# A hybrid decoder layer on one core: a new order of the seven block products, and the attention groups combined inside the attention stages

## The chip, the cores and the metric

The kernel runs on one core of a Trainium2 chip. The metric is the device time of one execution in microseconds. Before the change it is 3054.38 us, the median of three runs (3054.3 to 3061.18).

## What is computed

The reference is one decoder layer over a prompt of 2048 tokens and over eight sample sequences of one new token each, with model width 1024. After an RMS norm, one input projection feeds two branches, which are merged by sigmoid gates, projected and added to the residual:

```
h = rms_norm(x)
for g, (win, dil) in enumerate(((128, 1), (512, 4), (2048, 16))):   # 8 heads of 64 each
    q, k, v = cols(h, w_in, ...)            # 512 columns each
    o[g], lse[g] = dilated_attn(q, k, v, win, dil, alibi_slopes[g])   # 129 keys per query
mix = softmax over g of lse                 # per position and head
att = sum_g mix[g] * o[g] * silu(cols(h, w_in, OFF_ATT_GATE, 512))
# HGRN2 branch, 8 heads: q, f, i, gate of 1024 columns each
S_t = diag(f_t) S_{t-1} + k_t i_t^T;   o_t = S_t^T q_t     (evaluated in chunks)
ho = rms_norm(o) * silu(gate)
merged = ga * (att @ w_att_proj) + gb * (ho @ w_hg_proj)   # ga, gb: sigmoid of 1024 columns each
y = rms_norm(x + merged @ w_out)
```

All of it is float32. New keys and values, the HGRN state and the sample outputs are returned too.

## The kernel before

**Products.** A float32 operand is split into two parts of a faster type, `hi` and `lo` (`split_w`: ScalarE writes `hi`, VectorE subtracts to get `lo`), and a product is three matmuls per 128 rows of depth: hi*hi, hi*lo and lo*hi. On top of that each projection is a two-by-two block product done with seven block products instead of eight. The 1024 rows of depth are the two blocks of one side. The tokens of a half (1024) are split in two 512s, and two column groups are the blocks of the other side. `ORDER` names the seven combinations of the token side (`A11`, `S1`, `S2`, `A12`, `S3`, `S4`, `A22`; all seven stay in SBUF for a half), `w_combos` makes the seven of the weight side from four raw tiles and one difference tile (`wr`, five buffers). So product i multiplies `ORDER[i]` with `W[i]`. Before, the order is P1, P5, P6, P2, P7, P3, P4, where P1 + P2 is the first result block and the other three need sums of partial results that are kept aside.

**Two layouts.** `nat_block` computes values and HGRN inputs with tokens on the partitions (two accumulator banks for each of the three tags `pa`, `pb`, `pc`). The kept partial sums are copied by ScalarE (`keep_c`, tile `cc`), the results are added by VectorE or copied by ScalarE into `vst` and stored (`nat_fin`). `t_pair` computes everything else with columns on the partitions, two groups of 128 columns at a time, with one bank for each tag; tags `pa` and `pb` change places from one column block to the next (`flip`). In the first half (p = 0) a pair runs as two column blocks of 256 and 260 tokens (the four extra are sample tokens), in the second (p = 1) as one of 512. Both blocks of a pair use the same seven weights `W`. `open_T(slots, raws)` sets how many split weights the pool holds: 7 in the first half, 5 in the second.

**Stages.** Natural blocks of the first half; `att_stage(0)`, `cb_stage(0)`, `hg_stage(0)`; the token side of the second half is loaded and split; natural blocks of the second half, with the whole sample attention and sample HGRN state work handed in between the products (`mid`); then `att_stage(1)`, `cb_stage(1)`, `hg_stage(1)`, and two output stages.
- `att_stage` runs over four pairs of heads j and three groups g. `att_proj` projects q and k (a `t_pair`); `att_side` of the pair before does scores, Exp, transposes and the weighted values, and stores the outputs with their maxima and denominators to `natt[g][j]` in DRAM. Its score tiles `sc` have three buffers.
- `cb_stage` runs the two gate pairs (`att_gates`, Sigmoid, stored to `gs_scr`) and two merge-gate pairs (`merge_pair`), and for each j `combine`: it loads the three groups (`na`, 512 positions a tile), computes the softmax weights over the groups on VectorE with one Exp on ScalarE, scales and adds. `combine_T` transposes the result on TensorE, multiplies it by the gate read back from `gs_scr` (tile `gc`) and stores it to `att_scr`.
- `hg_stage` alternates per head a pair for f and q (`hg_fq`, with `hg_decay` behind it), the chunk recurrence of the head before (`hg_side`) and a pair for the gates.

**What sets the order.** The program is written in the order above, but a scheduler orders each engine's instructions: it goes by priority, which is program order unless `high_priority` lifts it (the weight splits of the next pair are lifted), and lets a later instruction go first where an earlier one would wait for data, a buffer or a bank. The order it finds is fixed; each engine then takes its queue in order. All loads and stores of these stages are issued from SyncE's queue. Buffers of a tag are given to a new tile when the old one's last reader is done.

Of the kernel before, what the change touches and what calls it, by code (L numbers as in the profile page):

```python
# [10 lines left out]
F32 = mybir.dt.float32  # L11
# [7 lines left out]
P = 128  # L19
# [23 lines left out]
HC = HALF // P  # L43
SW = 512 + NS // 2
SETS = (((0, 256), (256, 260)), ((0, 512),))
ORDER = ("A11", "S1", "S2", "A12", "S3", "S4", "A22")
C_IDENT, C_STEPS, C_STEPS2, C_CAUSAL, C_ONES, C_SEL, C_W = 0, 128, 384, 512, 640, 768, 776


# [27 lines left out]
def body(ctx, tc, x_p, x_s, c128, c512, c2048, st_in, norm_w, w_in, w_ap, w_hp, w_out, hg_nw, lbl, fin_w,  # L77
# [7 lines left out]
    sto = nc.sync.dma_start  # L85
# [146 lines left out]
    def w_combos(pl, raws, width, bufs, slots):  # L232
        def slot(src):
            return w_slot(pl, src, width, slots)

        b11, b21, b12, b22 = raws[0, 0], raws[1, 0], raws[0, 1], raws[1, 1]
        w0 = slot(b11)
        t3 = pl.tile([P, 4, width], F32, name="wr", tag="wr", bufs=bufs)
        V.tensor_tensor(out=t3, in0=b22, in1=b12, op=ALU.subtract)
        V.tensor_tensor(out=b12, in0=b12, in1=b11, op=ALU.subtract)  # L240
        w1 = slot(b12)
        V.tensor_tensor(out=b11, in0=b22, in1=b12, op=ALU.subtract)
        w2 = slot(b11)
        w3 = slot(b21)
        w4 = slot(t3)
        V.tensor_tensor(out=b21, in0=b21, in1=b11, op=ALU.subtract)
        w5 = slot(b22)
        w6 = slot(b21)
        return [w0, w1, w2, w3, w4, w5, w6]
# [61 lines left out]
                sto(kv[o0:o0 + (2 - u0) * P].rearrange("(u p) c -> p u c", p=P), v[:, u0:])  # L311

    def nat_fin(wn, p, g, half, r, c, b, ps, add):
        v = wn.tile([P, 2, 256], F32, name="vst", tag="vst", bufs=2)
        vf = v.rearrange("p u c -> p (u c)")
        if add is None:
            A.copy(out=vf, in_=ps)
        else:
            V.tensor_tensor(out=vf, in0=ps, in1=add, op=ALU.add)
        nat_store(p, g, half, r, c, b, v)  # L320
# [7 lines left out]
    def nat_block(wn, p, g, half, mid=None):  # L328
        raws = w_raw(wn, nat_cols(g, half), 256, 5)
        if p == 0:  # L330
            nat_samp(wn, raws, g, half)
        W = w_combos(wn, raws, 256, 5, 3)

        def prod(ps, b, i, first):
            for u in range(2):
                nat_mm(ps[:, u * 256:(u + 1) * 256], Hh[ORDER[i]], Hl[ORDER[i]], *W[i],
                       slice((2 * b + u) * P, (2 * b + u + 1) * P), first and u == 0, True)

        def keep_c(ps):
            c = wn.tile([P, 512], F32, name="cc", tag="cc", bufs=4 + p)  # L340
            A.copy(out=c, in_=ps)
            return c

        pa, pb, pc = [[ps_proj(t) for _ in range(2)] for t in range(3)]
        cc = {}
        for i, t in enumerate((pa, pc, pa, pb, pa, pc, pa)):
            for b in range(2):
                prod(t[b], b, i, i in (0, 1, 3))
                if i < 3:
                    cc[i, b] = keep_c(t[b])  # L350
                else:
                    r, c, add = ((0, 0, 0), (1, 1, 1), (0, 1, 2), (1, 0, None))[i - 3]
                    nat_fin(wn, p, g, half, r, c, b, t[b], None if add is None else cc[add, b])
            for f in mid.pop(0) if mid else ():
                f()
# [43 lines left out]
    def t_pair(p, c0s, idx, evs, W=None):  # L399
        W = W or t_combos(c0s)  # L400
        pl = tp["p"]
        for off, n in SETS[p]:
# [15 lines left out]
            def keep_c(ps):  # L418
                c = pl.tile([P, 512], F32, name="cc", tag="cc", bufs=3)
                A.copy(out=c[:, 0:n], in_=ps[:, 0:n])  # L420
                return c
# [9 lines left out]

            prod(pa, 0, True)
            c1 = keep_c(pa)
            prod(pc, 1, True)
            c5 = keep_c(pc)
            prod(pa, 2)
            c2 = keep_c(pa)
            prod(pb, 3, True)
            fin(0, 0, pb, c1)
            prod(pa, 4)  # L440
            fin(1, 1, pa, c5)
            prod(pc, 5)
# [205 lines left out]
            if n < 6:  # L648
                a, b = na, score(n + 3)

    def att_gates(pl, p, j, sto=sto):
        def evac(j):
            def f(r, off, npr, ps, add):
                z = val(ps, add)
                gt = pl.tile([P, 512], F32, name="gm", tag="gm", bufs=3)[:, 0:npr]
                A.activation(out=gt, in_=z, func=AF.Sigmoid)
                V.tensor_tensor(out=gt, in0=z, in1=gt, op=ALU.mult)
                t0 = p * HALF + r * 512 + off
                sto(gs_scr[j][:, t0:t0 + npr], gt)
            return f  # L660

        t_pair(p, (OFF_G + j * P, OFF_G + (j + 1) * P), (48 + j, 49 + j), (evac(j), evac(j + 1)))

    def combine(cb, j, cs):
        pend = []
        for c in cs:
            na = cb.tile([P, 3, 4, 132], F32, name="na", tag="na", bufs=4)
            for g in range(3):
                dma(na[:, g], natt[g][j][c * 512:(c + 1) * 512].rearrange("(i u) c -> i u c", u=4))
            mx = cb.tile([P, 4, 2], F32, name="mx", tag="mx", bufs=2)  # L670
            w3 = cb.tile([P, 3, 4, 2], F32, name="w3", tag="w3", bufs=2)
            V.tensor_tensor(out=mx, in0=na[:, 0, :, 128:130], in1=na[:, 1, :, 128:130], op=ALU.min)
            V.tensor_tensor(out=mx, in0=mx, in1=na[:, 2, :, 128:130], op=ALU.min)
            for g in range(3):
                V.tensor_tensor(out=w3[:, g], in0=mx, in1=na[:, g, :, 128:130], op=ALU.subtract)
            A.activation(out=w3, in_=w3, func=AF.Exp)
            wd = cb.tile([P, 3, 4, 2], F32, name="wd", tag="wd", bufs=2)
            V.tensor_tensor(out=wd, in0=w3, in1=na[:, :, :, 130:132], op=ALU.mult)
            V.tensor_tensor(out=mx, in0=wd[:, 0], in1=wd[:, 1], op=ALU.add)
            V.tensor_tensor(out=mx, in0=mx, in1=wd[:, 2], op=ALU.add)  # L680
# [8 lines left out]
            pend.append((c, na))  # L689
        return j, pend  # L690

    def combine_T(cb, j, pend):
        for c, na in pend:
            pt = ps_side()
            for u in range(4):
                TE.transpose(pt[:, u * P:(u + 1) * P], na[:, 0, u, 0:128], ident)
            gt = cb.tile([P, 512], F32, name="gc", tag="gm", bufs=3)
            dma(gt, gs_scr[j][:, c * 512:(c + 1) * 512])
            V.tensor_tensor(out=gt.rearrange("p (i u) -> p u i", u=4), in0=pt.rearrange("p (u i) -> p u i", u=4),
                            in1=gt.rearrange("p (i u) -> p u i", u=4), op=ALU.mult)  # L700
# [128 lines left out]

    def cb_stage(p):  # L830
        with pool("cb") as cb:
            fill = [lambda j=j: att_gates(cb, p, j) for j in (0, 2)]
            fill += [lambda d=d: merge_pair(cb, p, d) for d in ((0, 2) if p == 0 else (2, 4))]
            for j in range(4):
                if fill:
                    fill.pop(0)()
                if j:
                    combine_T(cb, *pend)
                pend = combine(cb, j, (2 * p, 2 * p + 1))
            for f in fill:  # L840
                f()
            combine_T(cb, *pend)

    def hg_stage(p):
# [307 lines left out]
        return samp_hg_prep, samp_hg_calc, samp_hg_state, samp_hg_out, samp_hg_end  # L1152

    def att_stage(p):
        with pool("at") as at:
            pend = None
            for j in range(4):
                for g in range(3):
                    nxt = (p, j, g) + att_proj(at, p, j, g) if pend is None else None
                    if pend is not None:  # L1160
                        att_side(at, *pend)
                        nxt = (p, j, g) + att_proj(at, p, j, g)
                    pend = nxt
            att_side(at, *pend)

    alloc_H()
    with banks(6, ABC), pool("wn") as wn, right("px") as px:
# [72 lines left out]

    bk = banks(3, ABC)
    bk.__enter__()
    open_T(7, 5)
    att_stage(0)
    cb_stage(0)
    hg_stage(0)
# [243 lines left out]
```

## Time and profile before

| | |
|---|---|
| median of 3 runs | 3054.38 us |
| profiled execution, its own time | 3056.5 us |
| its span, first to last instruction | 3054.6 us |
| TensorE busy | 2884.6 us, 94% |
| TensorE weight loads busy | 2502.7 us, 82% |
| VectorE busy | 1851.9 us, 61% |
| ScalarE busy | 1468.7 us, 48% |
| mean granted clock of TensorE | 0.979 of full speed |
| moved by DMA | 357 MB, mean 117 GB/s |

In the rows below TensorE stands as PE, VectorE as DVE, ScalarE as ACT, SyncE as SP; L413 is line 413 of the kernel. Matmuls overlap: one takes 0.28 us from start to end, but the next starts 0.12 us after it, so busy time is not throughput. PEclk is the share of full speed (2.4 GHz) that was granted to TensorE, which runs at 2.4 or 1.2 GHz. A wait is put down to what came last before it ended.

### The profile page before, as it was taken

Reading aid. Unit: us, or ns where it says so; the run is one execution under the profiler, and the core shown is the slowest. Engines: PE = TensorE matmul, PEld = TensorE weight load, DVE = VectorE, ACT = ScalarE, POOL = GpSimd, SP = SyncE. Lnnn points to the kernel's source line nnn. Section 1 sums busy time; section 2 is a strip of 40 time slices with the busy share of each in tenths; the row PEclk is TensorE's granted clock in tenths of the full one; section 3 lists DMA queues with packets and bytes.
Section 4 is the critical chain, followed back from the end, with each engine's and each line's share of the span. In section 5 each row is a group of like instructions: output and inputs, shape, how many; then the busy total and the mean of one; then the engine's idle time right before and its main releaser. Section 6 shows DMA issues by size and latency. Waiting matters only on the chain. (4 is left out here: it accounts for less than half of the span.)

```text
span 3054.6 us, 54166 instructions
## 1 busy us (share of the span) xinstructions
PE 2884.6 (94%) x20318; PEld 2502.7 (82%) x20318; DVE 1851.9 (61%) x4603; ACT 1468.7 (48%) x3271; POOL 2.5 (0%) x8
## 2 busy tenths in 40 slices
PE   8998999998899999989979999999999999999999
PEld 7997878888898999888866676777788887899886
DVE  7454455557777777666345555558877777544443
ACT  6333454545576676532334444445677773311232
POOL 0000000000000000000000000000000000000000
PEclk9999999999999999999989999999999999999999
DMA  5453222215421222457753222326322224744542
GB/s 188 141 173 112 70 60 82 82 57 173 129 64 60 76 64 83 162 173 242 206 149 87 83 86 79 93 64 205 93 81 73 78 76 151 224 135 136 161 150 78
DMA packets 453362, 357.45 MB, mean 117 GB/s; under 512 B 28505, under 2 KB 411818, under 8 KB 452178
## 3 DMA queue, kind: packets, MB, share of 16 engines
q1 hardware_dynamic: 452482, 351.93, 38.2%
q8 instruction: 162, 2.65, 0.4%
q0 software_dynamic: 320, 1.05, 0.1%
q14 instruction: 110, 0.90, 0.1%
q10 hardware_dynamic: 288, 0.92, 0.1%
HBM read 241.06 MB, written 113.26 MB: 116 GB/s over the span
## 5 line engine op out<-in xcount | busy, mean ns | idle before, releaser
L193 ACT ACTIVATE wh<-wr 128x512 fp32r<-128x512 f32 (+1 forms) x543 | 366.5, 681 | 523.1 <-PE pb L415 196.5
L194 DVE TENSOR_TENSOR wl<-wr,wh 128x512 fp32r<-128x512 f32 (+1 forms) x543 | 405.5, 752 | 240.9 <-ACT wh L193 213.4
L413 PE MATMUL pc<-hhS,wh 128*128 128x256 f32 (+2 forms) x816 | 266.3, 326 | 5.1 <-PEq L1348 3.9
L415 PE MATMUL pc<-hlS,wh 128*128 128x256 f32 (+2 forms) x816 | 264.7, 324 | 0.0
L416 PE MATMUL pc<-hhS,wl 128*128 128x256 f32 (+2 forms) x816 | 264.0, 324 | 0.0
L413 PE MATMUL pa<-hhA,wh 128*128 128x256 f32 (+2 forms) x612 | 204.7, 335 | 24.9 <-ACT gm L707 7.6
L590 ACT ACTIVATE sc<-sc,stg 128x256 f32<-128x256 f32 (+2 forms) x384 | 171.6, 448 | 99.8 <-DVE stg L588 96.5
L413 PE MATMUL pb<-hhA,wh 128*128 128x260 f32 (+2 forms) x612 | 203.9, 333 | 9.6 <-ACT wh L193 4.4
L415 PE MATMUL pa<-hlA,wh 128*128 128x256 f32 (+2 forms) x612 | 200.8, 328 | 0.0
L416 PE MATMUL pa<-hhA,wl 128*128 128x256 f32 (+2 forms) x612 | 200.6, 328 | 0.0
L415 PE MATMUL pb<-hlA,wh 128*128 128x260 f32 (+2 forms) x612 | 200.3, 327 | 0.0
L416 PE MATMUL pb<-hhA,wl 128*128 128x260 f32 (+2 forms) x612 | 198.9, 325 | 0.0
L588 DVE CUSTOM_DVE_ANT_0 sc<-px,bt 128x256 f32<-128x256 f32 (+2 forms) x384 | 123.6, 352 | 124.1 <-PE px L585 39.0
L413 PEld LDWEIGHTS pc<-hhS,wh 128*128 128x128 f32 x816 | 155.1, 190 | 19.4 <-issue 6.9
L193 ACT ACTIVATE th<-ra 128x256 fp32r<-128x256 f32 (+1 forms) x148 | 57.3, 417 | 224.9 <-PE pp L1399 157.4
L415 PEld LDWEIGHTS pc<-hlS,wh 128*128 128x128 f32 x816 | 155.1, 190 | 12.1 <-issue 1.5
L416 PEld LDWEIGHTS pc<-hhS,wl 128*128 128x128 f32 x816 | 155.1, 190 | 11.4 <-issue 0.2
L413 PEld LDWEIGHTS pa<-hhA,wh 128*128 128x128 f32 x612 | 117.6, 192 | 37.6 <-ACT gm L707 9.1
L600 PE MATMUL px<-cm,sc 128*128 128x128 f32 (+1 forms) x600 | 131.1, 294 | 17.0 <-ACT sc L590 15.2
L413 PE MATMUL pb<-hhS,wh 128*128 128x260 f32 (+1 forms) x408 | 136.2, 334 | 8.8 <-ACT cc L420 8.8
L413 PE MATMUL pa<-hhS,wh 128*128 128x256 f32 (+1 forms) x408 | 137.5, 337 | 7.5 <-ACT cc L420 7.5
L416 PE MATMUL pa<-hhS,wl 128*128 128x256 f32 (+1 forms) x408 | 135.9, 333 | 0.0
(476 smaller groups left out, 8319.3 us busy)
## 6 DMA issues: line engine op xcount, KB each, us to landing
wr<-in_w_in SPq DMA_DIRECT2D x272, 256.0 KB
wr<-in_w_in SPq DMA_DIRECT2D x40, 512.0 KB
vt<-vscr SPq DMA_DIRECT2D x52, 256.0 KB
na<-natt SPq DMA_DIRECT2D x48, 264.0 KB
vscr<-vst SPq DMA_DIRECT2D x48, 256.0 KB
natt<-stg SPq DMA_DIRECT2D x32, 264.0 KB
xt<-in_x_prompt SPq DMA_DIRECT2D x16, 512.0 KB
iscr<-vst SPq DMA_DIRECT2D x32, 256.0 KB
```

The lines of the kernel that those rows point to most:

```text
L193: A.activation(out=hi, in_=raw, func=AF.Copy)
L194: V.tensor_tensor(out=lo, in0=raw, in1=hi.bitcast(F32), op=ALU.subtract)
L413: TE.matmul(o, wh[:, k], hi[:, k, off:off + n], start=(first and k == 0), stop=False, skip_group_check=True)
L415: TE.matmul(o, wh[:, k], lo[:, k, off:off + n], start=False, stop=False, skip_group_check=True)
L416: TE.matmul(o, wl[:, k], hi[:, k, off:off + n], start=False, stop=(k == 3), skip_group_check=True)
L588: V.tensor_tensor_reduce(out=sc[:, hx, 0:W], in0=spss[hx][:, 0:W], in1=bt[:, hx, BW - W:BW], scale=-0.125, scalar=3e38, op0=ALU.add, op1=A ...
L590: A.activation(out=sc[:, hx, 0:W], in_=sc[:, hx, 0:W], func=AF.Exp, scale=-1.0, bias=stg[:, u, 128 + hx:129 + hx], accum_out=stg[:, u, 130 ...
L600: TE.transpose(pt[0:kw, (hx * nw + w) * P:(hx * nw + w + 1) * P], sc[:, hx, w * kw:(w + 1) * kw], ident)
```

## The change

Three things change together.
1. The product order becomes P1, P2, P6, P5, P7, P3, P4, in `ORDER`, `w_combos`, `nat_block` and `t_pair`. The second product now completes the first result block, and its weight is a raw tile.
2. In the natural blocks the buffers are `cc` 4 and `vst` 2 + p (before `cc` 4 + p and `vst` 2).
3. The gate pairs and three of the four `combine` move from `cb_stage` into `att_stage`: gate pair 0 ahead of it, gate pair 2 at j = 2, the combination of j - 1 in two pieces at g = 1 and 2, each transposed one step later. `cb_stage` keeps two merge pairs and the combination of j = 3. In `att_stage` the gate and `gc` tiles take the buffers of `sc`; `na` has two buffers in the first half, one in the second. The split weights have five slots in both halves.

```diff
-ORDER = ("A11", "S1", "S2", "A12", "S3", "S4", "A22")
+ORDER = ("A11", "A12", "S2", "S1", "S3", "S4", "A22")
@@ w_combos
-        w1 = slot(b12)
+        w1 = slot(b21)
         V.tensor_tensor(out=b11, in0=b22, in1=b12, op=ALU.subtract)
         w2 = slot(b11)
-        w3 = slot(b21)
+        w3 = slot(b12)
@@ nat_fin
-        v = wn.tile([P, 2, 256], F32, name="vst", tag="vst", bufs=2)
+        v = wn.tile([P, 2, 256], F32, name="vst", tag="vst", bufs=2 + p)
@@ nat_block
-            c = wn.tile([P, 512], F32, name="cc", tag="cc", bufs=4 + p)
+            c = wn.tile([P, 512], F32, name="cc", tag="cc", bufs=4)
...
-        for i, t in enumerate((pa, pc, pa, pb, pa, pc, pa)):
+        for i, t in enumerate((pa, pb, pa, pc, pa, pc, pa)):
...
-                if i < 3:
+                if i in (0, 2, 3):
                     cc[i, b] = keep_c(t[b])
                 else:
-                    r, c, add = ((0, 0, 0), (1, 1, 1), (0, 1, 2), (1, 0, None))[i - 3]
+                    r, c, add = {1: (0, 0, 0), 4: (1, 1, 3), 5: (0, 1, 2), 6: (1, 0, None)}[i]
@@ t_pair
             prod(pa, 0, True)
             c1 = keep_c(pa)
-            prod(pc, 1, True)
-            c5 = keep_c(pc)
+            prod(pb, 1, True)
+            fin(0, 0, pb, c1)
             prod(pa, 2)
             c2 = keep_c(pa)
-            prod(pb, 3, True)
-            fin(0, 0, pb, c1)
+            prod(pc, 3, True)
+            c5 = keep_c(pc)
@@ att_gates, combine, combine_T: tag and buffers become arguments
-    def att_gates(pl, p, j, sto=sto):
+    def att_gates(pl, p, j, tag=("gm", 3)):
...
-    def combine(cb, j, cs):
+    def combine(cb, j, cs, nb=4):
...
-    def combine_T(cb, j, pend):
+    def combine_T(cb, j, pend, tag=("gm", 3)):
@@ cb_stage
-            fill = [lambda j=j: att_gates(cb, p, j) for j in (0, 2)]
-            fill += [lambda d=d: merge_pair(cb, p, d) for d in ((0, 2) if p == 0 else (2, 4))]
-            for j in range(4):
-                if fill:
-                    fill.pop(0)()
-                if j:
-                    combine_T(cb, *pend)
-                pend = combine(cb, j, (2 * p, 2 * p + 1))
-            for f in fill:
-                f()
+            merge_pair(cb, p, 2 * p)
+            pend = combine(cb, 3, (2 * p, 2 * p + 1))
+            merge_pair(cb, p, 2 * p + 2)
             combine_T(cb, *pend)
@@ att_stage
+        tag = ("sc", 3)
         with pool("at") as at:
-            pend = None
+            att_gates(at, p, 0, tag)
+            pend = done = None
             for j in range(4):
                 for g in range(3):
-                    nxt = (p, j, g) + att_proj(at, p, j, g) if pend is None else None
                     if pend is not None:
                         att_side(at, *pend)
-                        nxt = (p, j, g) + att_proj(at, p, j, g)
-                    pend = nxt
+                    if done is not None:
+                        combine_T(at, *done, tag)
+                        done = None
+                    if j and g:
+                        done = combine(at, j - 1, (2 * p + g - 1,), 2 - p)
+                    if (j, g) == (2, 0):
+                        att_gates(at, p, 2, tag)
+                    pend = (p, j, g) + att_proj(at, p, j, g)
             att_side(at, *pend)
+            combine_T(at, *done, tag)
@@ body
-    open_T(7, 5)
+    open_T(5, 5)
     att_stage(0)
```

## Rows read from the trace of the kernel before

**Rows 1.** The page, part 1: busy time of the engines.
```profile
span 3054.6 us, 54166 instructions
...
PE 2884.6 (94%) x20318; PEld 2502.7 (82%) x20318; DVE 1851.9 (61%) x4603; ACT 1468.7 (48%) x3271; POOL 2.5 (0%) x8
```

**Rows 2.** Windows: length; busy us of PE, PEld, DVE, ACT, POOL; PEclk; DMA.
```profile
87.00:257.00 170.00, 169.53 (x1453) 162.21 (x1453) 79.63 (x101) 57.81 (x92) 0.00 (x0) 1.00 0.46 147
...
288.00:688.00 400.00, 389.70 (x3313) 329.28 (x3314) 211.09 (x672) 194.25 (x590) 0.00 (x0) 0.99 0.24 70
688.00:802.00 114.00, 101.61 (x838) 96.66 (x839) 86.10 (x274) 64.37 (x146) 0.00 (x0) 0.94 0.52 161
802.00:858.00 56.00, 46.64 (x350) 45.58 (x349) 33.10 (x80) 33.33 (x65) 0.00 (x0) 0.91 0.29 89
858.00:1218.00 360.00, 335.68 (x2720) 328.18 (x2719) 276.84 (x768) 242.07 (x514) 0.00 (x0) 0.98 0.23 70
...
1320.00:1450.00 130.00, 115.43 (x875) 107.81 (x876) 86.74 (x117) 34.07 (x44) 0.00 (x0) 0.93 0.73 232
1450.00:1605.00 155.00, 129.04 (x1023) 115.75 (x1021) 66.33 (x123) 50.81 (x114) 0.00 (x0) 0.92 0.67 178
...
2037.00:2141.00 104.00, 97.95 (x514) 74.44 (x513) 75.86 (x213) 55.73 (x111) 0.00 (x0) 0.97 0.55 169
2141.00:2189.00 48.00, 43.11 (x180) 33.05 (x179) 38.46 (x92) 31.71 (x52) 0.00 (x0) 0.96 0.37 117
```

**Rows 3.** Waits of PE, whole span: who, for whom, us total, times, longest.
```profile
PE pa L324 <- ACT vst L317: 12.7, 4, 7.7
PE pa L324 <- ACT cc L341: 11.5, 3, 5.4
...
PE pa L413 <- ACT cc L420: 7.5, 6, 2.6
...
PE pa L324 <- DVE vst L319: 3.3, 2, 1.9
```

**Rows 4.** Waits of ACT, 1450 to 1605.
```profile
ACT sv L1115 <- DMA sv<-in_state_hgrn: 44.3, 6, 13.4
...
ACT vst L317 <- DMA iscr<-vst: 7.1, 1, 7.1
```

**Rows 5.** Lines of DVE, 700:815: count, busy us, mean ns, idle before.
```profile
L685 DVE TENSOR_TENSOR na<-na,w 128x512 f32<-128x512 f32 x24 | 15.6, 684 | 0.0
L699 DVE TENSOR_TENSOR gc<-px,gc 128x512 f32<-128x512 f32 x8 | 8.3, 1080 | 5.0 <-DMA gc<-gs 5.0
L688 DVE TENSOR_TENSOR na<-na 128x512 f32<-128x512 f32 x8 | 5.5, 687 | 0.0
...
L675 DVE TENSOR_TENSOR w<-mx,na 128x8 f32<-128x8 f32 x24 | 2.7, 151 | 0.1
...
L672 DVE TENSOR_TENSOR mx<-na 128x8 f32<-128x8 f32 x8 | 1.3, 158 | 0.0
```

**Rows 6.** Lines of ACT, 700 to 815.
```profile
L676 ACT ACT_TABLE_LOAD x7 | 9.0, 1283 | 0.1
```

**Rows 7.** Timeline, 955.5 to 958.6: start us, us, engine, line, operation, idle before.
```profile
955.67 0.28 PE L413 MATMUL pb<-hhA,wh 128*128 128x260 f32 x1
...
957.12 0.28 PE L413 MATMUL pc<-hhS,wh 128*128 128x260 f32 x1
...
957.20 0.63 ACT L193 ACTIVATE wh<-wr 128x512 fp32r<-128x512 f32 x1 [0.66 <-PE pb L415]
...
957.74 0.36 ACT L420 COPY cc<-pb 128x260 f32<-128x260 f32 x1
...
957.86 0.70 DVE L194 TENSOR_TENSOR wl<-wr,wh 128x512 fp32r<-128x512 f32 x1 [2.06 <-ACT wh L193]
```

**Rows 8.** Timeline of PE around 420.45 and 426.44.
```profile
420.45 0.60 PE L627 MATMUL px<-cm,ot 128*128 128x128 f32 x4
...
426.44 0.28 PE L413 MATMUL pb<-hhA,wh 128*128 128x260 f32 x1
```

More of the change, by code (lines that the diff above doesn't have):

```diff
@@ L654, in f @@
                 z = val(ps, add)
-                gt = pl.tile([P, 512], F32, name="gm", tag="gm", bufs=3)[:, 0:npr]
+                gt = pl.tile([P, 512], F32, name="gm", tag=tag[0], bufs=tag[1])[:, 0:npr]
                 A.activation(out=gt, in_=z, func=AF.Sigmoid)
@@ L662, in att_gates @@
         t_pair(p, (OFF_G + j * P, OFF_G + (j + 1) * P), (48 + j, 49 + j), (evac(j), evac(j + 1)))
-    def combine(cb, j, cs):
+    def combine(cb, j, cs, nb=4):
         pend = []
         for c in cs:
-            na = cb.tile([P, 3, 4, 132], F32, name="na", tag="na", bufs=4)
+            na = cb.tile([P, 3, 4, 132], F32, name="na", tag="na", bufs=nb)
             for g in range(3):
                 dma(na[:, g], natt[g][j][c * 512:(c + 1) * 512].rearrange("(i u) c -> i u c", u=4))
-            mx = cb.tile([P, 4, 2], F32, name="mx", tag="mx", bufs=2)
-            w3 = cb.tile([P, 3, 4, 2], F32, name="w3", tag="w3", bufs=2)
+            mx = cb.tile([P, 4, 2], F32, name="mx", tag="mx", bufs=min(nb, 2))
+            w3 = cb.tile([P, 3, 4, 2], F32, name="w3", tag="w3", bufs=min(nb, 2))
             V.tensor_tensor(out=mx, in0=na[:, 0, :, 128:130], in1=na[:, 1, :, 128:130], op=ALU.min)
@@ L676, in combine @@
             A.activation(out=w3, in_=w3, func=AF.Exp)
-            wd = cb.tile([P, 3, 4, 2], F32, name="wd", tag="wd", bufs=2)
+            wd = cb.tile([P, 3, 4, 2], F32, name="wd", tag="wd", bufs=min(nb, 2))
             V.tensor_tensor(out=wd, in0=w3, in1=na[:, :, :, 130:132], op=ALU.mult)
@@ L696, in combine_T @@
                 TE.transpose(pt[:, u * P:(u + 1) * P], na[:, 0, u, 0:128], ident)
-            gt = cb.tile([P, 512], F32, name="gc", tag="gm", bufs=3)
+            gt = cb.tile([P, 512], F32, name="gc", tag=tag[0], bufs=tag[1])
             dma(gt, gs_scr[j][:, c * 512:(c + 1) * 512])
```

## The prediction

> **What bounds the kernel now.** The page's busy shares come first: TensorE 2884.6 of a span of 3054.6 us [rows 1]. So a gain can only be TensorE time that is idle now, or time in which its clock is at 1.2 instead of 2.4 GHz. A table by stages comes next, because the share is a mean over stages with different limits. For a stretch I count as lost its length less TensorE's busy time, plus length x (1 - PEclk) for the clock [rows 2]. The first attention stage (288 to 688) loses 10.3 us idle in 400 and the clock hardly at all: it is full. Its combine stage (688 to 802) loses 12.4 idle + 6.8 by the clock = 19.2 of 114. The first 56 us of the HGRN stage after it lose 9.4 + 5.0 = 14.4, the rest of that stage 24.3 + 7.2 of 360. The natural-layout blocks of the second half (1320 to 1605) lose 14.6 + 26.0 = 40.6 idle and 9.1 + 12.4 = 21.5 by the clock: the worst place. The second combine stage loses 6.1 + 3.1 = 9.2, the start of HGRN behind it 4.9 + 1.9 = 6.8. Last, who TensorE waits for: in the natural blocks for ScalarE's copy of the third product into `cc` (11.5 us) and for the output tile `vst` (12.7 + 3.3 us) [rows 3]. In the first half the same blocks run full (87 to 257: 169.5 busy of 170) [rows 2]; they have no sample attention or sample state between them.
>
> **Product order in the natural blocks (second half).** Before, products 1, 2 and 3 are all kept, two tiles each, and five `cc` buffers hold them; the sixth copy waits until VectorE has added the fourth product to the first. Now the second product finishes the first pair, the four buffers are never short, and VectorE may lag by three products instead of one. The 11.5 us of `cc` waits go whole. What is late next is the output: `vst` has three buffers for two, and two of the eight tiles now leave early. But the copies into `vst` wait for stores to land (7.1 us once), and in the same stretch ScalarE waits 44.3 us for the loads of the HGRN state, with a DMA share of 0.67 to 0.73 [rows 2, 4]; the third buffer doesn't change that queue. I take a third of the 16.0 us. Of the 21.5 us lost to the clock I take 4, since the sample matmuls that thin out TensorE's work stay. Sum -21; bounds 0 (DMA sets the pace and the waits only move) and -38 (all waits and half the clock).
>
> **Combination out of the combine stages.** One `combine` of 512 positions costs VectorE, over eight: 15.6 (three scalings) + 5.5 + 5.5 (two additions, one row shown) + 13.5 (eight groups of tiny ones, the largest 2.7, the smallest 1.3) = 40.1, so 5.0 us each, and `combine_T` 1.04 us more [rows 5]. In the combine stage this lies on a VectorE that is busy 86.1 of 114 us [rows 2], between the evacuations that free TensorE's accumulators, and its Exp alternates with the gates' Sigmoid: three groups of table loads (the first, of 7, shown; two more of 4), 15 in all at 1283 ns, 19.2 us of ScalarE [rows 6]. Three quarters of the combines move away and with them most of these loads, since the attention stage runs Exp anyway. I take three quarters of the loss: -14 in the first half (bounds 0 and -19), -7 in the second (0 and -9). The HGRN start keeps the last `combine_T`, whose gate tile VectorE waits for (idle before L699) [rows 5], so only -4 of 14.4 there (0 to -14), nothing in the second half (0 to -7).
>
> **What the attention stages get.** Per half two gate pairs, which the combine stage loses (no change in products), six `combine`, six `combine_T`, 18 `na` loads, six gate loads and six stores on SP's queue. VectorE goes from 211.1 to 211 + 6 x 6.0 = 247 busy of 400 us, before the gates come in [rows 2]; the `na` transfers find a DMA share of 0.24. Nothing of it is on TensorE except 24 transposes that were there before. The price is order: VectorE takes its queue in order, and behind a `combine_T` that waits for its gate tile stand the score steps of the attention side and all evacuations. The eight `combine_T` of the first combine stage waited 5.0 us in all, 0.6 each [rows 5]; twelve would wait 7.5, half of it covered by products in TensorE's queue: 4 us. The gate and `gc` tiles now take `sc` buffers, three in all, that the score steps need until a store has landed; in the second half `na` has one buffer, so its load waits for the transposes of the last one and SP's queue behind it too. For both together 4 us. Sum +8; bounds 0 (no product disappears, so no gain) and +31 (twelve waits of 2.6, half the 5.0 us).
>
> **Five weight slots instead of seven in the first half.** This is the dear part. A pair of columns there runs as two column blocks of seven products, with the same seven split weights, so all seven are live at once. With five slots the weights of products 6 and 7 can be split only after the second block has used up an earlier one: TensorE must run the second block's first product (its accumulator is free, because the second product now ends early), then products 6 and 7 of the first block. A product of twelve matmuls takes 957.12 - 955.67 = 1.45 us [rows 7]. From its end the next split weight is ready at 957.86 + 0.70 - 957.12 = 1.44 us, and the copy of the accumulator, which stands behind the split on ScalarE, at 0.98 us. So after the second block's first product TensorE has nothing for about 1.0 us: the block's third product waits for the copy, and by its end the sixth weight is there; its own slot then gives the seventh while product 6 runs. There are 34 pairs (12 attention, 2 gate, 4 merge, 16 HGRN). In the attention pairs the side work ends before the fourth product: after the last side transposes at 420.45 the block's remaining products fill 5.6 us alone [rows 8], and so it is for the sides of two groups in three. I count a full hole for 14 pairs (8 attention, 2 without a side, one gate, 3 merge), half for the 16 of HGRN, whose next side can start early, none for the other 4: 14 + 8 = +22. Bounds: 0 (other work covers it), and two weights uncovered in every pair, 2 x 1.44 x 34 = +98. I stay near the low end because the nearest row, the copy, is 1 us and the holes fall where ScalarE is not full.
>
> By the Trainium skill (Perfetto Trace Analysis, section Identifying the Most-Contended Engine) a gap that repeats on the engine that should be saturated can mean too few buffers for the next tile. No row of before shows such a gap for the weights, with seven slots. By that rule this term is nearer its upper bound, the second rival below.
>
> **The accumulator `pb`.** It is now written by the second product, one product after the last block's last evacuation instead of three. Such one-product waits exist already: `pa` waits for its copy 7.5 us in six places over the kernel [rows 3]. +3; bounds 0 and 0.37 us of a copy in each of 102 blocks, +38.
>
> **Sum.** -21 - 14 - 7 - 4 + 8 + 22 + 3 = -13 us. The profiled execution took 3056.5 us (1.9 us more than its span), the median shown is 2.1 below it. 3056.5 - 13 = 3043.5, against the median 3042 us.
>
> **The rivals.**
> First, the holes are covered: the scheduled order lets the second block start inside side work, and the attention side absorbs VectorE's new work. For it: TensorE's order already mixes blocks where it waits, and full stages lose little [rows 2]. Against: eight attention pairs end in products alone [rows 8]. The slot term falls to 4, the attention term to 3: -13 - 18 - 5 = -36, 3019 us.
> Second, on the other side, the slots decide. Both late weights lie open, in the 14 pairs whole (2 x 1.44 = 2.9 us, 41 us), in the 16 of HGRN by half (23 us): 64 instead of 22, the sum +29, 3083 us. For it: raw weights too are held longer, so the next pair's loads start later, and ScalarE in HGRN is busy 242.1 of 360 us [rows 2]. Against: the measured chain needs only one hole. The kernel gets slower than before from 35 us of holes on, 1.0 us as a mean over all 34 pairs; slower than can be told from no change from 44.
> Third, DMA sets the pace of the natural blocks: the waits for `cc` and `vst` come back as waits for weights or sample tiles, and of the -21 only 4 stay: -13 + 17 = +4, 3058 us. For it: 44.3 us of ScalarE's waits are for loads [rows 4]. Against: DMA is not full, and TensorE's waits there name no load.
>
> **How the numbers follow.** Forecast 0.42, first rival 0.24, second 0.20, third 0.14. A difference under 0.3% (9 us) can't be told from no change for this kernel: faster means under 3045, slower over 3063. The forecast's own spread of +-15 us puts 0.6 of it under 3045 and nearly all the rest into the middle; the first rival is faster, the second slower, the third mostly in the middle: faster 0.49, same 0.26, slower 0.25. The range of 8 in 10 reaches from 3016, past the first rival, to 3076, short of the second; the forecast's own range is 3027 to 3057.
>
> **What would show it.** Right: the natural blocks of the second half without TensorE waits for `cc` and with fewer for `vst`; the combine stages down to two pairs with under 5 us lost; table loads there gone; in the first half one gap of about 1 us per pair, at a product of the second block that waits for ScalarE's `cc`, or at weights `wh`, `wl`. Wrong: gaps over 2 us per pair at the weights (second rival); none (first rival); TensorE in 1320 to 1605 idle for 40 us still, behind other names (third). If the attention stages grow by more than 8 us beyond their holes and their gate pairs, the term for VectorE's order was mis-sized.

## The result and the profile after

The changed kernel takes 3098.88 us, the median of four runs (3091.96 to 3099.83), against 3054.34 for the kernel before on the same chip. The ratio is 1.0135, 95% interval 1.012 to 1.015: slower by 41 us by that ratio (the medians differ by 44.5). The forecast was 3042 (3016 to 3076), so even the sign was wrong. The profiled execution took 3091.96 us.

The page of the kernel after, part 1, answers to [rows 1]:
```profile
span 3090.2 us, 54105 instructions
...
PE 2907.3 (94%) x20318; PEld 2505.0 (81%) x20318; DVE 1852.6 (60%) x4603; ACT 1464.8 (47%) x3272; POOL 2.5 (0%) x8
```
The same 20318 matmuls keep TensorE busy for 22.7 us more, and of the span's 35.6 us only 12.9 are added idle time. So the share of busy time, 94% both times, says nothing here. The windows must, now cut where the same number of block-product matmuls has run, so that each stretch holds the same products in every kernel (first half: attention and combine, HGRN; second half: natural blocks with the merge pair ahead of them, attention and combine, HGRN; the two merge pairs behind the first HGRN stage, 52 to 56 us, are left out). The kernel before:
```profile
263.30:802.20 538.90, 514.73 (x4329) 448.09 (x4329) 315.15 (x983) 269.41 (x757) 0.00 (x0) 0.97 0.31 93
802.20:1248.10 445.90, 412.19 (x3316) 402.95 (x3314) 333.40 (x913) 291.62 (x615) 0.00 (x0) 0.97 0.24 73
1300.60:1604.50 303.90, 263.14 (x1989) 238.68 (x1987) 163.33 (x255) 94.00 (x172) 0.00 (x0) 0.93 0.67 194
1604.50:2140.90 536.40, 523.15 (x3132) 377.23 (x3133) 309.42 (x836) 263.05 (x679) 0.00 (x0) 0.99 0.33 99
2140.90:2550.10 409.20, 396.13 (x1993) 324.63 (x1992) 322.00 (x779) 293.69 (x520) 0.00 (x0) 0.99 0.27 80
```
The kernel after, columns as in [rows 2]:
```profile
263.80:804.00 540.20, 522.18 (x4329) 445.97 (x4330) 317.39 (x981) 259.07 (x747) 0.00 (x0) 1.00 0.33 94
804.00:1278.40 474.40, 431.95 (x3314) 409.95 (x3313) 331.93 (x911) 288.56 (x618) 0.00 (x0) 0.97 0.22 66
1333.60:1635.10 301.50, 258.56 (x1989) 236.29 (x1987) 163.77 (x258) 94.63 (x174) 0.00 (x0) 0.93 0.66 196
1635.10:2163.10 528.00, 517.04 (x3137) 374.93 (x3137) 317.57 (x865) 258.00 (x678) 0.00 (x0) 0.99 0.35 103
2163.10:2583.30 420.20, 398.12 (x1992) 324.33 (x1991) 313.34 (x750) 307.75 (x529) 0.00 (x0) 0.99 0.25 75
```
The loss is in HGRN: +28.5 in the first half, +11.0 in the second. The natural blocks, where I expected the largest gain, give 2.4 us. The second half's attention gains 8.4, the first half's nothing.

Waits of TensorE after, whole span, which answer to [rows 3]:
```profile
PE px L923 <- ACT kn L918: 22.4, 7, 3.3
PE pc L413 <- ACT wh L193: 14.4, 30, 0.6
...
PE pa L324 <- DVE vst L319: 8.6, 2, 5.6
PE pa L324 <- ACT wh L193: 8.4, 1, 8.4
PE pa L413 <- ACT kt L850: 8.3, 6, 1.7
PE pb L413 <- DVE cc L456: 7.4, 9, 1.1
PE px L767 <- DVE scs L761: 7.1, 1, 7.1
PE pa L324 <- ACT vst L317: 6.6, 2, 5.5
...
PE pa L324 <- ACT cc L341: 5.4, 2, 3.3
...
PE pc L416 <- DVE wl L194: 3.6, 13, 0.7
```
New are a wait for a weight in 30 of the 34 pairs of the first half (14.4 + 3.6 us), one for `kt` in six heads of the second half, and waits for `pb` behind VectorE's sums (`cc` L456). The first line, `kn`, is not new: it was 17.4 us in the same stage before. The waits for `cc` and `vst` in the natural blocks fell from 27.5 to 20.6, but 5.8 of that is back at `scs`.

### The profile page after: what moved, and what is told of

It reads as the page before. It is cut to its first block, busy times and chain, and to the rows that moved or that the text cites. A ratio compares the mean times of both kernels' runs of the same rounds, so it can differ in the third digit from the quotient of the medians.

```text
span 3090.2 us, 54105 instructions
## 1 busy us (share of the span) xinstructions
PE 2907.3 (94%) x20318; PEld 2505.0 (81%) x20318; DVE 1852.6 (60%) x4603; ACT 1464.8 (47%) x3272; POOL 2.5 (0%) x8
## 5 line engine op out<-in xcount | busy, mean ns | idle before, releaser
L413 PE MATMUL pc<-hhS,wh 128*128 128x256 f32 (+2 forms) x816 | 269.4, 330 | 21.1 <-ACT wh L193 14.4
L415 PE MATMUL pc<-hlS,wh 128*128 128x256 f32 (+2 forms) x816 | 263.5, 323 | 0.0
L413 PEld LDWEIGHTS pc<-hhS,wh 128*128 128x128 f32 x816 | 154.3, 189 | 44.3 <-ACT wh L193 21.5
L413 PEld LDWEIGHTS pb<-hhA,wh 128*128 128x128 f32 x612 | 116.5, 190 | 35.8 <-DVE cc L456 9.7
L415 PE MATMUL pa<-hlS,wh 128*128 128x256 f32 (+1 forms) x408 | 136.4, 334 | 0.0
```

The source lines that it names most:

```text
L413: TE.matmul(o, wh[:, k], hi[:, k, off:off + n], start=(first and k == 0), stop=False, skip_group_check=True)
L415: TE.matmul(o, wh[:, k], lo[:, k, off:off + n], start=False, stop=False, skip_group_check=True)
```

## The experiments

The first table gives each run's ratio to the kernel before on the same chip, with its 95% interval; the second the stage lengths of its profile in us, cut as above. "Order" is parts 1 and 2 of the change together.

| run | what | ratio | interval |
|---|---|---|---|
| e2_o7 | order | 0.9994 | 0.9983 to 1.0005 |
| e3_s5 | five slots | 1.0178 | 1.0164 to 1.0192 |
| e7_c7 | combination | 0.9966 | 0.9950 to 0.9982 |
| e1_oc7 | order, combination | 1.0035 | 1.0023 to 1.0048 |
| e4_c5 | combination, five slots | 1.0123 | 1.0108 to 1.0139 |
| e6_o5 | order, five slots | 1.0183 | 1.0159 to 1.0207 |
| e8_o6 | order, six slots | 1.0065 | 1.0047 to 1.0084 |
| e5_o7r | order, banks rotated | 1.0002 | 0.9989 to 1.0014 |
| e9_light_old | before, few sample loads | 0.9852 | 0.9835 to 0.9870 |
| e10_light_new | order, few sample loads | 0.9874 | 0.9853 to 0.9894 |
| e12_late_dve | after, late weights on VectorE | 1.0067 | 1.0052 to 1.0081 |
| e11_mix | order outside HGRN, combination | 0.9947 | 0.9931 to 0.9964 |

| | att. 1st | HGRN 1st | natural | att. 2nd | HGRN 2nd |
|---|---|---|---|---|---|
| before | 538.9 | 445.9 | 303.9 | 536.5 | 409.2 |
| after | 540.2 | 474.4 | 301.4 | 528.0 | 420.2 |
| e2_o7 | 529.1 | 447.5 | 302.3 | 527.7 | 416.7 |
| e3_s5 | 562.8 | 473.1 | 311.5 | 532.3 | 410.2 |
| e7_c7 | 539.9 | 436.5 | 305.4 | 532.8 | 405.6 |
| e1_oc7 | 542.3 | 449.3 | 305.2 | 529.5 | 420.3 |
| e4_c5 | 555.8 | 467.9 | 309.1 | 531.9 | 403.9 |
| e6_o5 | 551.2 | 482.7 | 301.7 | 528.7 | 417.6 |
| e8_o6 | 542.1 | 451.6 | 306.7 | 530.4 | 417.8 |
| e5_o7r | 531.7 | 452.5 | 303.2 | 528.5 | 413.8 |
| e9_light_old | 538.1 | 448.5 | 258.6 | 531.7 | 406.8 |
| e10_light_new | 526.7 | 448.7 | 265.4 | 527.8 | 417.8 |
| e12_late_dve | 536.1 | 464.5 | 301.7 | 528.2 | 420.0 |
| e11_mix | 544.7 | 437.8 | 305.4 | 529.6 | 404.8 |

Stages scatter: the natural blocks of kernels in which they are alike differ by up to 8 us from one profile to the next. The expectations of the first four runs cut HGRN elsewhere: 417 and 445 there are 446 and 474 here (the last pair is now in), 436 and 447 in the second half are 409 and 420.

**The three parts apart.** First the order alone, slots alone, and each pair of parts.
```diff
@@ e1_oc7, on the kernel after (first half)
-    open_T(5, 5)
+    open_T(7, 5)
-                        done = combine(at, j - 1, (2 * p + g - 1,), 2 - p)
+                        done = combine(at, j - 1, (2 * p + g - 1,), 1)
@@ e2_o7, on the kernel before: parts 1 and 2 of the change alone
@@ e3_s5, on the kernel before
-    open_T(7, 5)
+    open_T(5, 5)
@@ e4_c5, on the kernel after: parts 1 and 2 of the change undone
```


> The changed kernel with seven weight slots in the first half instead of five (the room comes from one buffer for the combined groups in the first half's attention stage too). In the profiles the first half's HGRN stage grew by 28 us (416.8 to 445.0) and the second half's, where the slots did not change, by 12 (435.5 to 447.4). Theory S (the slots decide): the 28 us go, and a few us per attention pair with them; about 3060 us, HGRN stage of the first half near 420. Theory O (the new product order loses in pairs with a side, through the accumulator that is written again one product after its evacuation): the HGRN stages stay near 440 and 447, the time near 3092. Theory C (the combination in the attention stages loses there what it gains): no change to speak of, 3095 to 3100; one buffer fewer may cost a few us more.

> The kernel before with the new product order alone (and its cc and vst buffers); seven slots, the combination in the combine stages as before. Theory S: only the second half shows anything: -2.5 in the natural blocks (as the profile after), up to +12 in HGRN there; 3054 to 3065 us, HGRN of the first half at 417. Theory O: HGRN of both halves grows, +28 and +12, 3085 to 3092 us. Theory C: within 5 us of 3054.

> The kernel before with five weight slots instead of seven in the first half and nothing else. Theory S: the first half's HGRN stage grows from 417 to about 445, the attention pairs by 1 to 2 us each; 3054 + 28 + 12 to 24 = 3094 to 3106 us. My forecast's term was +22: 3076. Theory O and theory C: under +10, 3054 to 3064.

> The kernel after with the old product order and the old natural buffers: the combination moved and five slots, no new order. Theory S: it keeps the first half's loss and loses HGRN's second half no more: 3099 - 12 + 2.5 = about 3090 us, HGRN 445 and 436. Theory O: HGRN back at 417 and 436, the gain of the combination shows (-8.4 in the second half's attention and combine stages): about 3045. Theory C: 3095 to 3100 still.

The slots decide. Alone they cost 1.78%, 54 us, more than the whole change and more than theory S itself had for that run (3094 to 3106, measured 3113.43); giving seven back takes the change to +0.35%. In the second half, where the slots do not change, HGRN keeps +7.5 with the order alone and is free of it without (403.9 in e4_c5). So the order does cost something in HGRN. It gains that back in the attention and combine stages, which no theory had: 0.9994 is no difference.

**Slots beside the order, six slots, combination alone.**
```diff
@@ e6_o5 and e8_o6, on e2_o7
-    open_T(7, 5)
+    open_T(5, 5)    # e8_o6: open_T(6, 5)
@@ e7_c7, on e4_c5
-    open_T(5, 5)
+    open_T(7, 5)
-                        done = combine(at, j - 1, (2 * p + g - 1,), 2 - p)
+                        done = combine(at, j - 1, (2 * p + g - 1,), 1)
```


> The product order with five slots, the combination as before: what the combination adds is the changed kernel less this one. Slots with the old order cost 55 us (ratio 1.0178: attention and combine stages of the first half +24, HGRN there +27, natural blocks +8). If the order lets the sixth and seventh weight follow sooner (the second block's second product can run before they are there), the attention part of it falls to some +5 while HGRN keeps +25: about 3088, and the combination is worth about -0 to +10 in the changed kernel. If the order changes nothing on the slots: 3054 + 55 - 2 = 3107 and the combination is worth -8.

> The product order with six slots, combination as before. By my forecast's chain only the seventh weight is late then, and its slot comes free after the second block's first product, whose 1.45 us just cover the 1.44 us that a weight takes: the holes go, about 3056. If what five slots cost is not the hole but the order that they force on everything queued behind the late splits (the next pair's weights too), half of the loss stays with six: about +15 in HGRN of the first half (460) and 3070 to 3080.

> The combination alone: old product order, seven slots, one buffer for the combined groups in both halves. My forecast had -14 -7 -4 +8 = -17 for it: 3037. Beside the order it measured +11 us (ratio 1.0035 with both against 0.9994 with the order alone). If the combination and the order gain the same thing (the waits in the combine stages), this kernel is faster than before, by about 5 to 8, and the two together give less than their sum. If the combination loses in the attention stages by itself: +8 to +12, 3062 to 3066, with the first half's attention and combine stages above 545.

The order changes little on the slots: five cost 58 us with it (1.0183 against 0.9994), 54 with the old one, which agree within their intervals. One slot fewer costs 22 us, and my chain had that one free; it falls in the attention stages (+13), not in HGRN as the other reading of e8_o6 had it (+4). The combination is worth -10 us alone, -17 beside five slots with the old order (1.0123 against 1.0178) and -15 with the new one (1.0135 against 1.0183), near the -17 forecast. Beside the new order with seven slots it costs 12 us instead (1.0035 against 0.9994): there the first half's attention and combine stages go from 529.1 back to 542.3.

**What a late weight does.** In the kernel after, timeline: start, us, engine, line, operation:
```profile
1019.45 0.28 PE L416 MATMUL pb<-hhA,wl 128*128 128x260 f32 x1
...
1019.57 0.27 PE L914 MATMUL px<-cm,kt 128*128 128x128 f32 x1
...
1019.65 0.63 ACT L193 ACTIVATE wh<-wr 128x512 fp32r<-128x512 f32 x1 [0.37 <-PE pb L415]
1019.68 0.39 PE L912 MATMUL px<-qt,kt 128*128 128x128 f32 x2
...
1020.18 0.36 ACT L420 COPY cc<-pb 128x260 f32<-128x260 f32 x1
1020.31 0.69 DVE L194 TENSOR_TENSOR wl<-wr,wh 128x512 fp32r<-128x512 f32 x1
...
1020.33 0.39 PE L413 MATMUL pc<-hhS,wh 128*128 128x256 f32 x1 [0.16 <-ACT wh L193]
```
The second block's first product ends its issue at 1019.45. Only then does ScalarE begin the sixth weight, behind it comes the copy of the accumulator, and TensorE goes on at 1020.33: the chain of the forecast, 0.9 us long. The hole looks cheap, because chunk products of HGRN (`px`) fill most of it. With the new order TensorE stands longer at a later place. Once per head it comes to the chunk's `kn`, which ScalarE copies behind the decay's Ln and Exp, and has nothing left to run. That the products used up in the holes are what is missing there is argued; no run moves them alone. TensorE's waits of HGRN's first half with seven slots (e2_o7), then with five (e6_o5):
```profile
PE px L930 <- ACT kn L925: 10.8, 7, 2.3
```
```profile
PE px L930 <- ACT kn L925: 22.4, 7, 3.3
...
PE pb L413 <- DVE cc L456: 6.8, 7, 1.1
```
And behind this standing TensorE's clock falls. Windows of e6_o5 around one such wait, which ends at 939.13:
```profile
929.00:939.00 10.00, 6.81 (x55) 6.39 (x54) 7.84 (x28) 9.90 (x17) 0.00 (x0) 1.00 0.28 79
939.00:942.40 3.40, 3.27 (x16) 3.27 (x16) 2.30 (x12) 1.72 (x7) 0.00 (x0) 0.51 0.00 0
942.40:952.00 9.60, 8.64 (x73) 8.30 (x73) 8.59 (x29) 5.35 (x15) 0.00 (x0) 1.00 0.23 64
```
PEclk is 0.51 for 3.4 us behind the wait: 1.2 instead of 2.4 GHz. In e6_o5 this comes back every 58 to 62 us with all seven waits (2.5 us the first, 3.3 the others), for 3.4 or 6.8 us, and begins at or just before their ends. With seven slots six of the seven waits there are 1.4 us, and the clock stays up behind them. It does not follow every time: in the kernel after, one of the six waits of 3.3 us (it ends at 1041.78) leaves the clock at 1.00, and in e8_o6 none of six waits of 2.5 us is followed by a fall. The stage (e2_o7, then e6_o5, there with the attention and combine stages ahead of it):
```profile
793.30:1240.80 447.50, 416.39 (x3319) 398.18 (x3318) 329.39 (x915) 287.86 (x617) 0.00 (x0) 0.99 0.24 73
```
```profile
262.70:814.00 551.30, 524.36 (x4329) 445.32 (x4330) 313.65 (x979) 265.42 (x751) 0.00 (x0) 1.00 0.31 90
814.00:1296.60 482.60, 435.49 (x3313) 412.65 (x3313) 333.55 (x913) 288.85 (x619) 0.00 (x0) 0.96 0.23 67
```
TensorE's idle time grows from 31.1 to 47.1, and the clock takes 482.6 x 0.04 = 19 us instead of 4: together 31 of the stage's 35.

With the old order the same loss comes about otherwise. The wait for `kn` in HGRN's first half of the kernel before, then the stage in e3_s5 and TensorE's waits in it:
```profile
PE px L930 <- ACT kn L925: 17.4, 7, 2.5
```
```profile
826.80:1300.00 473.20, 425.82 (x3316) 406.01 (x3315) 333.09 (x914) 292.18 (x617) 0.00 (x0) 0.98 0.23 68
```
```profile
PE px L930 <- ACT kn L925: 17.0, 7, 2.6
PE pb L413 <- DVE cc L456: 13.4, 8, 2.1
PE pc L413 <- ACT wh L193: 5.9, 10, 0.9
```
The wait for `kn` is there with seven slots already and does not grow, and the clock does not fall (0.97, then 0.98). Still the stage is 27 us longer: idle time grows by 13.7 us, at VectorE's sums of the accumulators (`cc` L456, 15.5 us in all against 1.1) and at the late weights (8.8 against none), and busy time by 13.6. These two waits are what both orders share (10.2 and 11.8 us in e6_o5). The stall at `kn` is the new order's: with seven slots it had shortened that wait from 17.4 to 10.8, and with five the wait is 22.4.

In the attention and combine stages (first line of e6_o5, 529.1 long with seven slots) idle time grows by 5.5 us, and the other 17 lie in TensorE's busy time at full clock. Part of it is the view: a matmul counts as busy for 0.28 us though the next could start after 0.12, so each hole shows 0.16 us too short. The start times in the two traces divide these 17. There are 34 more holes (91 against 57), which hide 5.5 us. Behind every hole at a block product, and behind part of the changes from one product to another, the second matmul starts some 0.21 us after the first instead of 0.12 (behind 1020.33 above the next starts at 1020.55): 230 times against 162, 6.7 us more. And starts that are late by less than 0.16 us where TensorE goes over from one product to another come to 5.4 us more.

**Is it the split on ScalarE?** A late weight's `hi` part goes to VectorE.
```diff
 e12_late_dve (on after), weights six and seven of the first half's pairs:
-        A.activation(out=hi, in_=raw, func=AF.Copy)
+        V.tensor_copy(hi, raw)
```


> The changed kernel (five slots) with the hi parts of the sixth and seventh weight written by VectorE instead of ScalarE in the first half's column pairs. With five slots ScalarE stands longer at these two splits (waits for TensorE 80 us in the attention and combine stages against 46 with seven), and the copies behind it come later: TensorE's wait for kn in HGRN is 22.4 us against 10.8. Theory Q (the queue behind the split): those waits go back, HGRN of the first half falls from 474 to 455 to 462, the time by 10 to 25 us from 3099. Theory H (the hole itself: two splits that cannot start before TensorE is done with the slot): nothing changes or it gets worse, as VectorE takes 68 copies more (0.4 to 0.7 us each): 474 to 485, 3099 to 3115.

1.0067 against 1.0135: 20 us come back, as theory Q said, and theory H is refuted; HGRN falls to 464.5, a little less far than the 455 to 462 of theory Q, and the attention and combine stages by 4.1. The profile (TensorE's waits from 263.5 to 1264.1) shows the 13.3 us of `pc` for `wh` gone (the 6.0 of `pa`, 5.9 in the kernel after, are another wait), `kn` shorter, and some of the hole now at the copy `cc`:
```profile
PE px L926 <- ACT kn L921: 17.7, 7, 2.5
PE pa L416 <- ACT wh L196: 6.0, 2, 5.4
PE pc L416 <- ACT cc L423: 4.9, 10, 0.5
PE pb L416 <- ACT cc L423: 4.5, 9, 0.9
```
The copy is 426 ns on VectorE against 627 on ScalarE, and no engine stands between `hi` and `lo`; how much of the gain is that and how much the freed queue, this run cannot tell.

**What the natural blocks wait for.** Most sample loads are left out (the same arithmetic runs on the first ones).
```diff
 e9_light_old (on before), e10_light_new (on e2_o7)
-            dma(kc, cache_rows(g, n, 0))
-            dma(qb, qs_scr[g][n:n + 1].to_broadcast([P, AW]))
+            if n == 0:    # both into tiles of their own; sv and ib likewise, if h == 0
```


> The kernel before with most of the sample loads of the second half's natural blocks left out: 21 of 24 loads each of cache keys and of broadcast queries, and 7 of 8 loads each of HGRN states and broadcast inputs; the same arithmetic runs on the first ones, so the sample outputs are not the reference's. It is the partner of the next run. If the loads set the pace there, the stage falls from 303.9 us to 270 to 285; if the buffers of the partial results do, its waits for cc (11.5) and vst (16.0) stay and it falls by less than 10.

> The same loads left out of the kernel with the product order alone (seven slots). With all loads the order changed that stage by -1.6 us (303.9 to 302.3; TensorE idle 40.8 to 44.2), where my forecast had -21. If the loads hid the gain (my third rival), the stage is 10 to 20 us shorter here than in the run before this one. If the order gains nothing there whatever the loads, because cc and vst wait for ScalarE's and VectorE's queues and not for buffers, the two stages differ by less than 4.

The stage in e9_light_old, then in e10_light_new:
```profile
1302.00:1560.60 258.60, 246.54 (x1989) 225.66 (x1987) 160.88 (x256) 94.58 (x172) 0.00 (x0) 0.98 0.50 157
```
```profile
1291.30:1556.70 265.40, 245.74 (x1988) 225.41 (x1986) 161.92 (x252) 95.62 (x175) 0.00 (x0) 0.98 0.49 153
```
With the old order and the old buffers the stage falls by 45 us, idle time from 40.8 to 12.1, and these are all waits of TensorE over 0.3 us in it:
```profile
PE pa L324 <- ACT wh L193: 5.3, 1, 5.3
PE pb L413 <- ACT wh L193: 4.5, 1, 4.5
PE pc L325 <- DVE wl L194: 1.0, 1, 1.0
PE pa L325 <- DVE wl L194: 0.5, 1, 0.5
PE px L811 <- DMA vc<-in_cache_kv_w: 0.4, 1, 0.4
```
No wait of TensorE for `cc` or `vst` is left, with the old buffers: the loads made them. ScalarE still waits 17.2 us for a `cc` buffer there, but TensorE no longer stands behind it. By which way the loads did it, ScalarE's own wait for the HGRN state (44.3 us) or stores that land late among the loads (7.1 us once) [rows 4], this run cannot tell, as it takes away both. Neither branch of the second expectation came true: with the loads out of the way the new order is 6.8 us longer (one wait for the first weight, 10.7 instead of 5.3), neither 10 to 20 shorter nor within 4, and within the scatter of this stage. It shows no gain by the order.

**Why the order costs HGRN.** The banks are rotated so that the second product's bank has two products' time to be evacuated.
```diff
 e5_o7r (on e2_o7)
-            tp["flip"] = 1 - f
+            tp["flip"] = (f + 1) % 3
-            pa, pb, pc = ps_proj(f), ps_proj(1 - f), ps_proj(2)
+            pa, pb, pc = ps_proj(f), ps_proj(f + 1), ps_proj(f + 2)
```


> The kernel with the product order alone (seven slots, combination as before), and the three accumulator banks rotated from block to block: the second product takes the bank of the last block's fifth and sixth, the fourth product the bank of its last. The second product then follows two products after the evacuation of its bank, not one. Theory B (the one-product slack is what HGRN loses by the order, in the second half TensorE's wait of 1.3 us per gate pair for ScalarE's two Sigmoids): HGRN of the second half falls from 416.7 to about 409, the gains of the order in the attention and combine stages (529.1 and 527.7 against 538.9 and 536.5 before) stay: about 8 us under the order alone, ratio to before 0.995 to 0.997. Theory E (the sequence of the evacuations itself costs it, whatever the bank): HGRN stays at 415 to 418, ratio 0.999.

TensorE's waits in the second half's HGRN, order alone, then rotated:
```profile
PE pa L413 <- ACT kt L857: 7.8, 6, 1.3
...
PE pb L413 <- ACT kt L857: 2.5, 1, 2.5
...
PE px L930 <- ACT kn L925: 1.0, 1, 1.0
```
```profile
PE px L930 <- ACT kn L925: 7.3, 7, 1.1
PE pc L413 <- ACT cc L420: 3.8, 2, 3.0
```
Theory B names the wait rightly: the second product waits for the two Sigmoids of the block before, and rotated the wait is gone. But 6.3 us more are waited at `kn` (6.6 us in the kernel before), the stage falls by 2.9 (413.8) and not by 8, HGRN of the first half grows by 5.0, and the kernel gains nothing. So the bank accounts for 2.9 of the 7.5 us that the order costs here; the cause of the rest stays open.

**A version that beats both.** HGRN keeps the old order, everything else takes the new; the combination is in the attention stages, with seven slots and one `na` buffer.
```diff
 e11_mix (on e1_oc7): t_pair, t_combos, w_combos get old=False, and
+ORDER2 = ("A11", "S1", "S2", "A12", "S3", "S4", "A22")    # old=True: hg_fq, hg_gate
```


> Combination in the attention stages with seven slots (ratio 0.9966 with the old order, 1.0035 with the new), and the new order everywhere except in the pairs of the HGRN stages, which keep the old one. If the order loses in the HGRN pairs alone (445.9 to 447.5 and 409.2 to 416.7 with the order by itself; 436.5 to 449.3 and 405.6 to 420.3 beside the combination): HGRN back to about 437 and 406, attention and combine of the second half at 529 and not 533: 3040 to 3046, ratio 0.995 to 0.997. If order and combination disturb each other in the attention stages: ratio about 1.000, HGRN still above 440.

3044.03 us against 3058.6, ratio 0.9947: faster than the kernel before by 16 us by that ratio, and than the changed one by 1.9%. Against e1_oc7 HGRN is 11.5 and 15.5 us shorter, so beside the combination the order costs 27 us there. Against e7_c7 (0.9966) the intervals overlap; the order's gain outside HGRN is at most small.

## Why the prediction was wrong

**"Five weight slots": +22, measured +54 with the old order and +58 with the new.** This step failed by most. The place was right: a wait for the weight in 30 of 34 pairs, with a chain of 0.9 us where the forecast had about 1.0; with the waits for `wl` they sum to 18.0 us. What failed is the cover, and with it the price of a hole. HGRN's 16 pairs were counted by half, "whose next side can start early", 8 us, and four pairs at nothing. HGRN lost 27 us with the old order and 35 with the new. Side work does fill most of the hole there, but TensorE then stands elsewhere: at VectorE's sums of the accumulators in both orders, and with the new order 11.6 us more at `kn`, with 15 us of clock beside it. The other part, at most 14 us in the forecast, lost 24 and 22 us in the attention and combine stages, most of it in short holes and restarts that show as busy time. The rule of the Trainium skill (Perfetto Trace Analysis, section Optimization Strategy; the prediction names the section ahead of it), that a gap which repeats on the engine that should be saturated can mean too few buffers, pointed the right way. The repeating gap was there, with seven slots (e1_oc7) it is gone, and 58 lies nearer to the second rival's 64 than to 22.

**"Product order in the natural blocks": -21, measured -1.6 to -2.5.** That is inside the scatter of the stage. I read the `cc` and `vst` waits as a lack of buffers and gave DMA only part of `vst`. The row that spoke against it stood beside them [rows 4]: ScalarE, which makes these copies, waits 44.3 us for the HGRN state. Likewise "the sample matmuls that thin out TensorE's work stay": they stay in e9_light_old, and the granted clock rises from 0.93 to 0.98. It was the loads.

**"The accumulator pb": +3.** Mis-sized: the order alone costs 7.5 us in HGRN's second half, where the bank behind two Sigmoids explains 2.9 of them (e5_o7r), and 27 in both halves beside the combination. A gain I had not seen, -9.8 and -8.8 in the two attention and combine stages, cancels the 7.5 with the order alone. In the first half it is mostly clock (PEclk 0.97 before, 0.99 with the order), and it does not add to the combination's gain (e1_oc7).

**Combination: -14 - 7 - 4 + 8 = -17, measured -10 alone and -15 in place.** Near in sum, not in its places, so this is partly luck; and beside the new order with seven slots it costs 12. In e7_c7 the first half's attention and combine stages, priced at -14 and half of the +8, gain nothing together (+1.0); HGRN after them gains 9.4, and the second half 3.7 + 3.6.

**The rivals.** The second (slots 64, not 22) and the third (-4 of -21 stays) both came near in size, and I had priced them as alternatives: together 3056.5 - 13 + 42 + 17 = 3102.5, against 3091.96 in the profiled run and a median of 3098.88. For the second this is luck: its sign, gaps over 2 us per pair at the weights, is not there (the longest is 0.7). The third has its sign: the stage stays idle for 42.9 us, part of it behind other names, and the loads are shown as the cause.

What stays open: what the order costs HGRN beyond the bank; why the combination and the order do not add up with seven slots; and whether the longer waits at `kn` come from the products that had filled the holes, which no run moved alone.

## What to carry to other kernels

A buffer taken away from a loop that was full costs more than the waits that name it: here 18 us of waits for weights stood for 54 to 58 us, the rest as waits at later copies, restarts that show as busy time and, with the new order, a lower clock. Look for it at the next in-order places, and time such a part alone before it goes into a sum. Before adding buffers for a tile that is waited for, look at what the engine that writes the tile waits for itself. Rivals that can come true together are priced together. Parts of a change that each gain alone can lose together: run them in pairs.

## What was not expected of the hardware

With each of the seven stalls of 2.5 to 3.3 us at `kn` in e6_o5, TensorE went to 1.2 GHz for 3.4 or 6.8 us; six stalls of 1.4 us at the same place in e2_o7 had no such fall. The fall is not certain: one stall of 3.3 us in the kernel after and six of 2.5 us in e8_o6 left the clock up. In the natural blocks, the granted clock went from 0.93 to 0.98 when loads were left out and the matmuls stayed the same. Behind every hole at a block product, and behind part of the changes of product, the second matmul started some 0.21 us after the first instead of 0.12; five slots brought 68 more of these in the first half's attention and combine stages (e6_o5 against e2_o7), 6.7 us that no wait shows.
